# Second-norm adaLN columns on two engines, down projections one up tile later, and unread value products in a two-layer hybrid transformer kernel

## The chip, the cores and the metric

One core of a Trainium2 chip runs the whole program in one launch. The metric is the device time of an execution in microseconds. Before the change three runs took 1842.49, 1840.63 and 1834.53 us: median 1840.63.

## What is computed

One inference step of a diffusion backbone with two layers, for 128 context tokens and 512 latent tokens of width 1024, all in float32. Cut to what matters here, a layer is

```python
sa, ca, ga, sf, cf, gf = silu(cond) @ w_ada + b_ada     # six vectors of 1024, for context and for latents
h = rmsnorm(x) * g_mix * (1 + ca) + sa
q, ckv, krope, qd, kd, vd, u = split(h @ w_in)          # latent attention, differential attention, Fourier
o = concat(mla(q, ckv, krope), diff(qd, kd, vd), fourier(u)) @ w_out
x = x + ga * o
h = rmsnorm(x) * g_ffn * (1 + cf) + sf                  # the second norm
gate, val = split(conv3(h @ w_up))
x = x + gf * (silu(gate) * val) @ w_down
```

In `w_ada` the 6 x 1024 outputs are 48 columns of 128. Columns 0 to 7 are the shift `sa`, 8 to 15 the scale `ca`, 16 to 23 the gate `ga`, 24 to 31 the shift `sf` of the second norm, 32 to 39 its scale `cf`, 40 to 47 the gate `gf`.

## The kernel before

Activations lie feature-major, as tiles of 128 features by up to 646 tokens. A float32 product is made of three matmuls (`mm3`, L130 to L133): both operands are split into a rounded high part and the rest. `weight` (L117 to L125) loads a block of weights through SP's DMA queue into a tile `raw`, of which two rotate, lets ScalarE (ACT) cast the high half (`whi`, L112) and VectorE (DVE) or GpSimd (POOL) subtract the low half (`wlo`, L113). A tile scheduler orders each engine's instructions by priority when the program is built; the engines then run their lists in order. Work under `later(FILL)` has low priority and is placed late, where others leave room.

A layer runs through these stages. `norm_first`, `diff_k` and `diff_q` make the first projections. `diff_v` (L452) makes the values of differential attention: four blocks of weights i, each against five token groups t, into three PSUM tiles `vps`; in the last block each finished group is split into high and low halves `VVd` (ACT cast L431, subtraction L432). The heads follow in a hand-written order, the string `SEQ` (L1058): `d` and `m` are heads, `F` is the Fourier mixing (names `fc`, `fcc`, `fp`, `fpc`), `w0` and `w1` load the first two blocks of `w_out`, and each `g` is one adaLN column on TensorE (PE).

An adaLN column is made in one of three ways. `ada_pe` (L165) loads the column's weights into a `raw` tile and makes eight plain float32 matmuls of 128 columns (`ada2p`, L170; two columns are needed, they are repeated 64 times). `ada_dve` (L146) loads them in another layout into an `ada` tile and makes two multiply-and-sum passes on DVE (L149) and an addition (L152). `ada_pool` (L156) multiplies on POOL (L159), sums on ACT (L160) and adds on DVE (L161). In layer 0 the columns 16 to 23 are the `g` of the heads.

`ffn` (L895) begins with the out projection. For two halves of the tokens and eight blocks m of `w_out` it makes 24 matmuls `wo`, adds the result to x (`residual`, L862) and its squares to `acc_x` for the norm. In layer 0 `step` sends the sixteen columns 24 to 39 along with the blocks, by turns as `ada_dve` and `ada_pool` (`ADA2_ENG`), in numbers given by `ADA2_STEP`. When a half is through, `stats` makes its norm (`rsh`, `rb`), `make_gain` (L177) turns the scale columns 32 to 39 into `gain`, and `modulate` normalises the half (`nt`, `hh_o`, `hl_o`).

Then come 22 up tiles j. Each has two blocks of weights and two halves, 96 matmuls `up`, and a convolution on ACT and DVE (L987, L989), the gate on ACT and POOL, and the split `gh` (ACT), `gl` (POOL). Three further columns per up tile (40 to 47, and all of layer 1) run on DVE. The tiles form the groups `FGROUPS = ((0, 8), (8, 8), (16, 6))`; behind each group come its down products `dn` (L1003 to L1032), the last group's by halves.

```python
SEQ = ('... g g m00 . e2 m01 P m10 F p0 m11 p1 m20 w0 w1 m21 p2', ...)
ADA2_ENG = "VPVPVPVPVPVPVPVP"
ADA2_STEP = (0, 0, 0, 2, 2, 3, 3, 3, 3)
```

Of the kernel before, what the change touches and what calls it, by code (L numbers as in the profile page):

```python
# [21 lines left out]
P = 128  # L22
L = 2
# [22 lines left out]
def backbone_kernel(ctx: ExitStack, tc: tile.TileContext, A, O):  # L46
# [221 lines left out]
    def attention(l, xs, rb, close_x):  # L268
        with tc.tile_pool(name=f"at{l}", bufs=1, side="left", reuse_waits="tile") as ap, \
# [183 lines left out]
            def diff_v():  # L453
                vv = [vvt(f"VVd{p}") for p in range(NPAIR)]
                s0, s1, s2 = sct("vps0"), sct("vps1"), avt("vps2")
                ps = [s0[:, 0:384], s0[:, 512:896], s1[:, 0:384], s1[:, 512:896], s2[:, :384]]
                for i in range(4):
                    hi, lo = weight(A["w_v"][l, i], 768)
                    for t in range(5):
                        for k in (2 * i, 2 * i + 1):  # L460
                            c0 = 132 + 128 * t if t < 4 else 2
                            s = slice(c0, c0 + 128)
                            w = slice(384 * (k % 2), 384 * (k % 2) + 384)
                            mm3(ps[t], hh[k][:, s], hl[k][:, s], hi[:, w], lo[:, w], k == 0, k == NK - 1)
                        if i == 3 and t < 4:
                            v_split(vv, t, ps[t])
# [335 lines left out]
            gates = list(range(16, 24)) if l == 0 else []  # L802
# [88 lines left out]
    def ffn(l, oh, ol, ws):  # L891
        xs, accs, close = x_pool(f"x{l}")
        with tc.tile_pool(name=f"ff{l}", bufs=1, side="left", reuse_waits="tile") as fp, \
# [17 lines left out]
            def ada_list(js, xpool=None, engs=""):  # L911
                scond = ada_cond(fp.tile([P, 2, D], F32, name="scond", tag="scond"))
                junk = fp.tile([P, D], BF16, name="junk", tag="junk")
                if "P" in engs:
                    prod = xpool.tile([P, 2, D], F32, name="prod", tag="prod")

                def step(n):
                    for _ in range(min(n, len(js))):
                        ll, j = js.pop(0)
                        wt = (xpool if xpool and j % 2 else fp).tile([P, D], F32, name="ada", tag="ada", bufs=ADA_BUFS)  # L920
                        if engs[j - 24:j - 23] == "P":
                            ada_pool(ll, j, wt, scond, prod)
                        else:
                            ada_dve(ll, j, wt, scond, junk)
# [46 lines left out]
            for f0, nf in FGROUPS:  # L971
                G = []
                for j in range(f0, f0 + nf):
                    c = []
                    for gv in range(2):
                        wh, wl = weight3(A["w_up"][l, j, gv], 1024)
                        ct = gpl.tile([P, 2, 322], F32, name="cg" if gv == 0 else "cv", tag=f"c{gv}", bufs=2)
                        cw = wconv[:, j, gv]
                        for hf in range(2):
                            t = pst("up")[:, :324]  # L980
                            r = slice(322 * hf, 322 * hf + 324)
                            for k in range(NK):
                                s = slice(128 * k, 128 * k + 128)
                                mm3(t, wh[:, s], wl[:, s], hh[k][:, r], hl[k][:, r], k == 0, k == NK - 1)
                            d = ct[:, hf]
                            nc.scalar.activation(out=d, in_=t[:, 1:323], func=AF.Copy, scale=cw[:, 1:2])
                            nc.vector.scalar_tensor_tensor(out=d, in0=t[:, 0:322], scalar=cw[:, 0:1], in1=d,  # L987
                                                           op0=ALU.mult, op1=ALU.add)
                            nc.vector.scalar_tensor_tensor(out=d, in0=t[:, 2:324], scalar=cw[:, 2:3], in1=d,  # L989
                                                           op0=ALU.mult, op1=ALU.add)  # L990
                        c.append(ct)
                    nc.scalar.activation(out=c[0], in_=c[0], func=AF.Silu)
                    nc.gpsimd.tensor_tensor(out=c[0], in0=c[0], in1=c[1], op=ALU.mult)  # L993
                    gh = gpl.tile([P, 2, 322], F32R, name="gh", tag="gh", bufs=GV_BUFS)
                    gl = gpl.tile([P, 2, 322], F32R, name="gl", tag="gl", bufs=GV_BUFS)
                    hi_lo(gh, gl, c[0], nc.gpsimd)
                    G.append((gh, gl))
                    step(3)
                if f0 + nf == NFF:
                    step(48)  # L1000
                    if l + 1 < L:
                        make_gain(l + 1, 0)
                last = f0 + nf == NFF  # L1003
                for hs in ((0,), (1,)) if last else ((0, 1),):
# [17 lines left out]
                    if last:  # L1022
                        rb[hs[0]] = stats(hs[0], 321, [acc, sq], pool)
                        if l + 1 == L:
                            for k in range(NK):
                                y = pool.tile([P, 642], F32, name="y", tag="t640")
                                for o, w, c, r in rb[hs[0]]:
# [4 lines left out]
                                    nc.sync.dma_start(out=dst, in_=y[:, o:o + w])  # L1032
            if l + 1 < L:
# [14 lines left out]
ADA2_ENG = "VPVPVPVPVPVPVPVP"  # L1048
RAWX = 1
XL = 2  # L1050
ADA2_STEP = (0, 0, 0, 2, 2, 3, 3, 3, 3)
# [6 lines left out]
SEQ = ('q1 d00 d01 k2 q2 K0 B+ . g d10 A+ e0 . d11 g g n0 e1 g d20 K1 n1+ d21 . g n2+ g g . K2 U+ . g g m00 . e2 m01 P m10 F p0 m11 p1 m20 w0 w1 m21 p2', 'd00 q1 d01 k2 q2 K0 d10 g B+ . g g A+ e0 . K1 g d11 e1 n0 g n1+ d20 . n2+ . g K2 g . d21 U+ m00 . g g e2 P m01 m10 F m11 p0 m20 w0 w1 m21 p2 p1')  # L1058
# [66 lines left out]
def _layout(i):  # L1125
# [11 lines left out]
    o["w_ada0"] = wa[0].reshape(NK, P, 48, P).transpose(2, 1, 0, 3)[:24].reshape(24, P, D)  # L1137
# [62 lines left out]
```

## Time and profile before

| | |
|---|---|
| median of three runs | 1840.63 us (1834.53 to 1842.49) |
| profiled execution | 1835.91 us, its span 1834.1 us |
| PE busy, mean granted clock | 1702.3 us (93%), 0.959 |
| DVE, ACT, POOL busy | 1160.6, 779.4, 647.0 us |
| layer 0: value products | about 75 to 105 us |
| layer 0: out projection `wo` | 377.6 to 459.4 us |
| layer 0: up and down products | from 463.9 us |
| layer 1: value products, out projection's end | about 985 to 1015, 1343 us |

The profile is of one execution, and its times are counted from the start of its span. A matmul's listed duration is its latency, since matmuls overlap; the pace is the distance of their starts, or a count over a window. PEclk is the granted clock of TensorE as a share of 2.4 GHz, so 0.5 is its lower level of 1.2 GHz. The idle time in square brackets stands before an instruction, with what ended it. DMA times go from the issue to the landing of the last byte.

### The profile page before, as it was taken

What the parts mean: (1) busy time and instruction counts of PE and PEld (TensorE: products, weight loads), DVE (VectorE), ACT (ScalarE), POOL (GpSimd) and SP (SyncE); (2) the same over time, 40 slices, a digit from 0 to 9 for tenths busy, and PEclk for the clock granted to TensorE, in tenths of its full rate; (3) what the DMA queues carried; (4) which work ended last, traced back from release to release, by engine and by line L of the source; (5) the groups of instructions that cost most, each with busy time, mean ns of one, the idle gap of its engine ahead of it and who ended that gap; (6) DMA issues with size and microseconds to landing.
All of it is one profiled execution on the core that took longest, in us unless ns stands there. A gap on an engine that the chain in (4) does not pass through costs nothing. (4 is left out here: it accounts for less than half of the span.)

```text
span 1834.1 us, 29035 instructions
## 1 busy us (share of the span) xinstructions
PE 1702.3 (93%) x11160; PEld 1653.7 (90%) x11160; DVE 1160.6 (63%) x2051; ACT 779.4 (42%) x1494; POOL 647.0 (35%) x719
## 2 busy tenths in 40 slices
PE   5888899988899999999998888999999999999997
PEld 4878899878799999999987878988999999999997
DVE  8738775679899999634455388765544434443445
ACT  5436665653533123313344457665333313321332
POOL 6547454558432002201232566562312201220222
PEclk8889999998799999999999899999999999999998
DMA  7367754654355665322254566652312222222223
GB/s 276 108 204 216 206 168 135 210 186 160 109 168 173 194 197 172 93 81 70 64 180 142 162 206 192 190 194 64 104 35 81 70 78 72 71 80 70 78 69 119
DMA packets 81084, 249.70 MB, mean 136 GB/s; under 512 B 10417, under 2 KB 19761, under 8 KB 79281
## 3 DMA queue, kind: packets, MB, share of 16 engines
q1 hardware_dynamic: 74226, 209.13, 35.9%
q0 software_dynamic: 6720, 38.72, 7.6%
q8 instruction: 88, 1.44, 0.3%
q14 instruction: 50, 0.41, 0.1%
HBM read 203.43 MB, written 41.24 MB: 133 GB/s over the span
## 5 line engine op out<-in xcount | busy, mean ns | idle before, releaser
L132 PE MATMUL up<-hl_o,whi 128*128 128x324 f32 x1408 | 440.9, 314 | 3.9 <-POOL hl_o L113 3.9
L131 PE MATMUL up<-hh_o,whi 128*128 128x324 f32 x1408 | 440.1, 314 | 2.9 <-ACT hh_o L112 1.7
L133 PE MATMUL up<-hh_o,wlo 128*128 128x324 f32 x1408 | 440.2, 313 | 0.0
L112 ACT CAST whi<-raw 128x1024 fp32r<-128x1024 f32 (+2 forms) x210 | 207.0, 989 | 427.3 <-PE dn L132 201.8
L113 DVE TENSOR_TENSOR wlo<-raw,whi 128x1024 fp32r<-128x1024 f32 (+2 forms) x184 | 225.2, 1228 | 199.4 <-ACT whi L112 195.3
L993 POOL TENSOR_TENSOR cg<-cg,cv 128x644 f32<-128x644 f32 x44 | 72.2, 1640 | 666.9 <-DVE cv L989 646.2
L132 PEld LDWEIGHTS up<-hl_o,whi 128*128 128x128 f32 x1408 | 267.5, 190 | 5.9 <-POOL hl_o L113 5.8
L131 PEld LDWEIGHTS up<-hh_o,whi 128*128 128x128 f32 x1408 | 267.3, 190 | 3.5 <-ACT hh_o L112 2.1
L133 PEld LDWEIGHTS up<-hh_o,wlo 128*128 128x128 f32 x1408 | 266.7, 190 | 0.0
L131 PE MATMUL dn<-gh,whi 128*128 128x322 f32 x704 | 218.0, 313 | 4.8 <-ACT gh L112 3.7
L132 PE MATMUL dn<-gl,whi 128*128 128x322 f32 x704 | 219.8, 313 | 0.0
L133 PE MATMUL dn<-gh,wlo 128*128 128x322 f32 x704 | 218.5, 312 | 0.0
L149 DVE CUSTOM_DVE_ANT_0 junk<-ada,scond 128x1024 bf16<-128x1024 f32 x138 | 195.7, 1418 | 5.3 <-ACT scond L143 2.5
L480 DVE TENSOR_REDUCE nm<-sc 128x1 f32<-128x640 f32 (+1 forms) x180 | 126.5, 711 | 76.6 <-PE sc L579 54.9
L481 ACT ACTIVATE P<-sc,nm 128x640 f32<-128x640 f32 (+1 forms) x180 | 128.4, 715 | 81.9 <-DVE nm L480 60.3
L862 DVE SCALAR_TENSOR_TENSOR x_x<-dn,mods,x_x 128x128 f32<-128x128 f32 (+2 forms) x144 | 57.6, 436 | 130.6 <-PE dn L133 130.4
L131 PEld LDWEIGHTS dn<-gh,whi 128*128 128x128 f32 x704 | 132.6, 189 | 6.7 <-ACT gh L112 4.0
L132 PEld LDWEIGHTS dn<-gl,whi 128*128 128x128 f32 x704 | 133.6, 190 | 0.3 <-POOL gl L113 0.2
L133 PEld LDWEIGHTS dn<-gh,wlo 128*128 128x128 f32 x704 | 133.4, 190 | 0.4 <-DVE wlo L113 0.4
L131 PE MATMUL proj<-hh_n,whi 128*128 128x320 f32 (+1 forms) x320 | 108.7, 340 | 5.3 <-DVE VVm L654 2.5
L132 PE MATMUL proj<-hl_n,whi 128*128 128x320 f32 (+1 forms) x320 | 106.0, 331 | 0.0
L133 PE MATMUL proj<-hh_n,wlo 128*128 128x320 f32 (+1 forms) x320 | 105.6, 330 | 0.0
(299 smaller groups left out, 3706.9 us busy)
## 6 DMA issues: line engine op xcount, KB each, us to landing
raw<-in_w_up SPq DMA_DIRECT2D x88, 512.0 KB, 3.5
ada<-in_w_adaT SPq DMA_DIRECT2D x83, 512.0 KB, 3.7
raw<-in_w_down SPq DMA_DIRECT2D x32, 512.0 KB, 3.6
raw<-in_w_in SPq DMA_DIRECT2D x28, 512.0 KB, 4.5
raw<-in_w_down SPq DMA_DIRECT2D x32, 384.0 KB, 3.2
qs<-dq POOLq DMA_DIRECT2D x12, 865.5 KB, 9.0
ks<-mk POOLq DMA_DIRECT2D x12, 768.0 KB, 5.0
raw<-in_w_out SPq DMA_DIRECT2D x16, 512.0 KB, 4.1
```

Source lines behind the costliest of these rows:

```text
L112: nc.scalar.copy(out=hi, in_=src)
L113: (lo_eng or nc.vector).tensor_tensor(out=lo, in0=src, in1=hi.bitcast(F32), op=ALU.subtract)
L131: nc.tensor.matmul(out, lhsT=lh, rhs=rh, start=first, stop=False)
L132: nc.tensor.matmul(out, lhsT=lh, rhs=rl, start=False, stop=False)
L133: nc.tensor.matmul(out, lhsT=ll, rhs=rh, start=False, stop=last)
L149: nc.vector.tensor_tensor_reduce(out=junk, in0=wt, in1=scond[:, c], op0=ALU.mult, op1=ALU.add, scale=1.0, scalar=0.0, accum_out=mods[:, l, ...
L480: nc.vector.tensor_reduce(out=nm, in_=s_in, axis=ax, op=ALU.max, negate=True)
L481: nc.scalar.activation(out=p_out, in_=s_in, func=AF.Exp, bias=nm, scale=1.0, accum_out=s_out)
L862: nc.vector.scalar_tensor_tensor(out=x[:, o:o + w], in0=ps, scalar=gate, in1=x[:, o:o + w], op0=ALU.mult, op1=ALU.add)
L993: nc.gpsimd.tensor_tensor(out=c[0], in0=c[0], in1=c[1], op=ALU.mult)
```

## The change

The change has three parts.

The second norm's columns in layer 0: 24 to 31 (the shift) leave the out projection and become eight more `g` among the last heads, as `ada_pe`; the input `w_ada0` grows from 24 to 32 columns. 32 to 39 (the scale) stay with the out projection, now all as `ada_dve`, fewer per step. `ada_pool` is no longer called there.

The down products of a group, in both layers, come behind the first up tile of the next group. Those of the last group stay where they were.

In `diff_v`, both layers, seven matmuls of 128x512 whose result is never read (`warm`) stand ahead of the blocks i=2 and i=3. Their operands are the low half of the block before.

```diff
+    def warm(n, lhsT, rhs):
+        t = tpt("warm")[:, :rhs.shape[-1]]
+        for _ in range(n):
+            nc.tensor.matmul(t, lhsT=lhsT, rhs=rhs, start=True, stop=True)
...
+                lo = None
                 for i in range(4):
+                    if i > 1:
+                        warm(7, lo[:, :128], lo[:, :512])
                     hi, lo = weight(A["w_v"][l, i], 768)
...
-            gates = list(range(16, 24)) if l == 0 else []
+            gates = list(range(16, 32)) if l == 0 else []
...
-                    step = ada_list([(l, j) for j in range(24, 40)], wop, ADA2_ENG)
+                    step = ada_list([(l, j) for j in range(32, 40)], wop)
...
-            for f0, nf in FGROUPS:
-                G = []
-                for j in range(f0, f0 + nf):
...
-                if f0 + nf == NFF:
-                    step(48)
-                    if l + 1 < L:
-                        make_gain(l + 1, 0)
...
+            G = {}
+            for f0, nf in FGROUPS:
+                for j in range(f0, f0 + nf):
+                    G[j] = up(j)
+                    step(3)
+                    if j == f0 and f0:
+                        down(f0 - 8, 8, [G.pop(i) for i in range(f0 - 8, f0)])
+            step(48)
+            if l + 1 < L:
+                make_gain(l + 1, 0)
+            down(f0, nf, [G[i] for i in range(f0, NFF)])
...
-ADA2_ENG = "VPVPVPVPVPVPVPVP"
...
-ADA2_STEP = (0, 0, 0, 2, 2, 3, 3, 3, 3)
+ADA2_STEP = (0, 0, 0, 1, 1, 1, 1, 2, 2)
...
-... m00 . e2 m01 P m10 F p0 m11 p1 m20 w0 w1 m21 p2
+... m00 . e2 m01 P g g m10 g F p0 g m11 g p1 g m20 w0 w1 g m21 g p2
...
-    o["w_ada0"] = wa[0].reshape(NK, P, 48, P).transpose(2, 1, 0, 3)[:24].reshape(24, P, D)
+    o["w_ada0"] = wa[0].reshape(NK, P, 48, P).transpose(2, 1, 0, 3)[:32].reshape(32, P, D)
```

`up` and `down` hold the code of before, moved into functions. Where the scheduler put things shows in the built order of the engines. Line numbers of the changed kernel are 6 to 9 higher than before from `ada_dve` on.

PE at the end of layer 0's attention, first before, then changed. `av` and `avc` are the last head's products, `fp` is Fourier, `ada2p` adaLN columns, `wo` the out projection.

```order
L545 MATMUL av<-th,VVm_3083 128x256
L553 MATMUL avc<-th,VVm_3083 128x128
L546 MATMUL av<-tl,VVm_3083 128x256
L554 MATMUL avc<-tl,VVm_3083 128x128
L131 MATMUL wo<-hh_o_3462,whi 128x322
L132 MATMUL wo<-hl_o_3470,whi 128x322
L133 MATMUL wo<-hh_o_3462,wlo 128x322
```

```order
L133 MATMUL fp<-tb,yl 128x256
L131 MATMUL fp<-tb,rowh 128x256
L132 MATMUL fp<-tb,rowh 128x256
L133 MATMUL fp<-tb,rowl 128x256
L176 MATMUL ada2p<-c_condT,raw 128x128 x32
L131 MATMUL wo<-hh_o_3490,whi 128x322
L132 MATMUL wo<-hl_o_3498,whi 128x322
L133 MATMUL wo<-hh_o_3490,wlo 128x322
```

Four of the new columns (32 matmuls) and the last Fourier products now stand between the heads and the out projection. The other four stand among the last heads.

SP, the queue of loads, at the same place, first before, then changed. `raw<-in_w_out` are the weights of the out projection, `raw<-in_w_ada` those of columns on PE, `ada<-in_w_adaT` those of columns on DVE, `x_x` the residual.

```order
L121 DMA raw<-in_w_in 128x1024
L167 DMA raw<-in_w_ada 128x1024
L121 DMA raw<-in_w_out 128x1024
L641 DMA mk_170<-base 128x1x768 x2
L121 DMA raw<-in_w_out 128x1024 x3
L929 DMA x_x_4277<-in_xT 128x642
L929 DMA x_x_4278<-in_xT 128x642
```

```order
L933 DMA x_x_4396<-in_xT 128x642
L173 DMA raw<-in_w_ada 128x1024
L915 DMA wconv<-in_w_conv 128x132
L148 DMA scond<-in_cond 128x2048
L153 DMA ada<-in_w_adaT 128x1024 x2
L121 DMA raw<-in_w_out 128x1024
L153 DMA ada<-in_w_adaT 128x1024 x2
L173 DMA raw<-in_w_ada 128x1024
L121 DMA raw<-in_w_out 128x1024
L153 DMA ada<-in_w_adaT 128x1024 x3
L121 DMA raw<-in_w_out 128x1024
L173 DMA raw<-in_w_ada 128x1024
```

Before, four loads of `w_out` stood ahead of the residual's eight loads. Now all eight stand behind them, in turn with columns' loads, and the last column's load stands behind the second block of `w_out` through `raw`.

PE in `diff_v` at the last block of weights, first before, then changed.

```order
L133 MATMUL vps_669<-whi,hl_n_183 128x384
L131 MATMUL vps_669<-whi,hh_n_176 128x384
L132 MATMUL vps_669<-wlo,hh_n_176 128x384
L133 MATMUL vps_669<-whi,hl_n_184 128x384
L131 MATMUL vps_667<-whi,hh_n_177 128x384
L132 MATMUL vps_667<-wlo,hh_n_177 128x384
L133 MATMUL vps_667<-whi,hl_n_185 128x384
```

```order
L133 MATMUL vps_669<-whi,hl_n_183 128x384
L131 MATMUL vps_669<-whi,hh_n_176 128x384
L132 MATMUL vps_669<-wlo,hh_n_176 128x384
L133 MATMUL vps_669<-whi,hl_n_184 128x384
L139 MATMUL warm<-wlo 128x512 x7
L131 MATMUL vps_667<-whi,hh_n_177 128x384
L132 MATMUL vps_667<-wlo,hh_n_177 128x384
L133 MATMUL vps_667<-whi,hl_n_185 128x384
```

The seven unread matmuls stand ahead of the block's first product; the same is found ahead of i=2, and twice in layer 1.

## Rows read from the trace of the kernel before

**Rows 1.** The page, section 1: engine, busy us (share of the span), instructions.

```profile
PE 1702.3 (93%) x11160; PEld 1653.7 (90%) x11160; DVE 1160.6 (63%) x2051; ACT 779.4 (42%) x1494; POOL 647.0 (35%) x719
```

**Rows 2.** Windows: width; PE, PEld, DVE, ACT, POOL busy (count); PEclk, DMA, GB/s.

```profile
500.00:598.00 98.00, 98.00 (x659) 98.00 (x658) 98.00 (x159) 35.26 (x55) 23.68 (x14) 1.00 0.56 174
```

**Rows 3.** PE waits from 75, 985, 370, 500, 620: total, times, longest.

```profile
PE vps L131 <- DVE VVd L432: 3.9, 1, 3.9
...
PE vps L131 <- DVE VVd L432: 4.6, 1, 4.6
...
PE wo L133 <- DVE wlo L113: 5.8, 2, 3.3
...
PE dn L131 <- ACT gh L112: 3.7, 1, 3.7
...
PE dn L131 <- ACT whi L112: 0.6, 3, 0.2
```

**Rows 4.** Windows in the value products of layers 0 and 1.

```profile
80.00:90.00 10.00, 10.00 (x56) 9.66 (x55) 4.12 (x3) 2.84 (x3) 8.39 (x7) 1.00 0.88 243
100.00:105.00 5.00, 3.12 (x11) 2.64 (x11) 1.36 (x5) 2.29 (x8) 1.47 (x3) 0.65 0.93 352
1015.00:1020.00 5.00, 5.00 (x24) 5.00 (x25) 0.29 (x1) 0.79 (x4) 3.89 (x6) 0.67 0.51 158
```

**Rows 5.** PE in order of time, `wo`: start, us, operation [idle before].

```profile
377.62 0.36 PE L131 MATMUL wo<-hh_o,whi 128*128 128x322 f32 x1
...
459.12 0.30 PE L133 MATMUL wo<-hh_o,wlo 128*128 128x320 f32 x1
```

**Rows 6.** Windows in and behind the out projections of layers 0 and 1.

```profile
400.00:420.00 20.00, 16.69 (x93) 16.43 (x94) 20.00 (x21) 6.38 (x11) 17.55 (x9) 0.84 0.61 197
460.00:480.00 20.00, 12.71 (x42) 10.19 (x43) 15.15 (x38) 13.38 (x38) 15.20 (x20) 0.55 0.30 106
1340.00:1350.00 10.00, 6.97 (x40) 6.75 (x40) 6.64 (x15) 4.06 (x8) 1.61 (x2) 0.83 0.00 0
```

**Rows 7.** Window around the first down products of layer 0.

```profile
605.00:615.00 10.00, 7.55 (x40) 7.55 (x41) 9.01 (x14) 2.83 (x3) 3.38 (x2) 0.83 0.43 141
```

**Rows 8.** PE in order of time, value products of layer 0.

```profile
94.41 0.33 PE L133 MATMUL vps<-whi,hl_n 128*128 128x384 f32 x1
98.61 0.69 PE L131 MATMUL vps<-whi,hh_n 128*128 128x384 f32 x1 [3.87 <-DVE VVd L432]
...
102.30 0.52 PE L133 MATMUL vps<-whi,hl_n 128*128 128x384 f32 x1
```

**Rows 9.** ACT in order of time, same place.

```profile
95.78 1.04 ACT L112 CAST whi<-raw 128x1024 fp32r<-128x1024 f32 x1 [8.61 <-DMA raw<-in_w_in]
96.73 0.26 ACT L431 CAST VVd<-vps 128x128 fp32r<-128x128 f32 x1
```

**Rows 10.** PE in order of time, an adaLN column among the heads.

```profile
343.79 0.66 PE L170 MATMUL ada2p<-c_condT,raw 128*128 128x128 f32 x4
344.21 0.40 PE L131 MATMUL sc<-ks,qs 128*128 128x320 f32 x1
```

**Rows 11.** SP (DMA issues) in order of time, around the out projection.

```profile
344.48 6.34 SPq L121 DMA_DIRECT2D raw<-in_w_out  x2
...
382.00 2.27 SPq L121 DMA_DIRECT2D raw<-in_w_out  x3
```

**Rows 12.** DMA issues, whole span, then 375-392: KB, median us to landing.

```profile
raw<-in_w_up SPq DMA_DIRECT2D x88, 512.0 KB, 3.5
...
raw<-in_w_out SPq DMA_DIRECT2D x3, 512.0 KB, 7.1
```

**Rows 13.** Groups by line, 368-485: busy us, mean ns, idle before.

```profile
L159 POOL TENSOR_TENSOR prod<-ada,scond 128x1024 f32<-128x1024 f32 x16 | 46.9, 2944 | 0.8 <-ACT prod L160 0.8
...
L149 DVE CUSTOM_DVE_ANT_0 junk<-ada,scond 128x1024 bf16<-128x1024 f32 x23 | 37.9, 1647 | 2.6 <-ACT scond L143 2.5
```

**Rows 14.** DVE in order of time, end of the out projection.

```profile
461.11 0.57 DVE L161 TENSOR_SCALAR mods<-mods,c_b_ada 128x2 f32<-128x2 f32 x1 [3.47 <-ACT prod L160]
```

More of the change, by code (lines that the diff above doesn't have):

```diff
@@ L909, in pst, with ada_list @@
                 return pf.tile([P, 512], F32, name=nm, tag="f", bufs=6)
-            def ada_list(js, xpool=None, engs=""):
+            def ada_list(js, xpool=None):
                 scond = ada_cond(fp.tile([P, 2, D], F32, name="scond", tag="scond"))
                 junk = fp.tile([P, D], BF16, name="junk", tag="junk")
-                if "P" in engs:
-                    prod = xpool.tile([P, 2, D], F32, name="prod", tag="prod")
                 def step(n):
@@ L920, in step @@
                         wt = (xpool if xpool and j % 2 else fp).tile([P, D], F32, name="ada", tag="ada", bufs=ADA_BUFS)
[L921 to L924, printed above, removed]
+                        ada_dve(ll, j, wt, scond, junk)
                 return step
@@ L970, in ffn @@
             acc = accs()
-            for f0, nf in FGROUPS:
-                G = []
-                for j in range(f0, f0 + nf):
[L974 to L998, printed above, removed]
-                if f0 + nf == NFF:
-                    step(48)
-                    if l + 1 < L:
-                        make_gain(l + 1, 0)
@@ new lines, in up @@
+            def up(j):
+                c = []
+                for gv in range(2):
+                    wh, wl = weight3(A["w_up"][l, j, gv], 1024)
+                    ct = gpl.tile([P, 2, 322], F32, name="cg" if gv == 0 else "cv", tag=f"c{gv}", bufs=2)
+                    cw = wconv[:, j, gv]
+                    for hf in range(2):
+                        t = pst("up")[:, :324]
+                        r = slice(322 * hf, 322 * hf + 324)
+                        for k in range(NK):
+                            s = slice(128 * k, 128 * k + 128)
+                            mm3(t, wh[:, s], wl[:, s], hh[k][:, r], hl[k][:, r], k == 0, k == NK - 1)
+                        d = ct[:, hf]
+                        nc.scalar.activation(out=d, in_=t[:, 1:323], func=AF.Copy, scale=cw[:, 1:2])
+                        nc.vector.scalar_tensor_tensor(out=d, in0=t[:, 0:322], scalar=cw[:, 0:1], in1=d,
+                                                       op0=ALU.mult, op1=ALU.add)
+                        nc.vector.scalar_tensor_tensor(out=d, in0=t[:, 2:324], scalar=cw[:, 2:3], in1=d,
+                                                       op0=ALU.mult, op1=ALU.add)
+                    c.append(ct)
+                nc.scalar.activation(out=c[0], in_=c[0], func=AF.Silu)
+                nc.gpsimd.tensor_tensor(out=c[0], in0=c[0], in1=c[1], op=ALU.mult)
+                gh = gpl.tile([P, 2, 322], F32R, name="gh", tag="gh", bufs=GV_BUFS)
+                gl = gpl.tile([P, 2, 322], F32R, name="gl", tag="gl", bufs=GV_BUFS)
+                hi_lo(gh, gl, c[0], nc.gpsimd)
+                return gh, gl
@@ L1003, in ffn, with down @@
+            def down(f0, nf, G):
                 last = f0 + nf == NFF
```

2 lines of the change are left out of this document (1 added, 1 removed).

## The prediction

> **What bounds the kernel.** I read the page's shares first, then TensorE's waits, then the stages that hold them in windows and in order of time. PE is busy 93% of the span [rows 1] at a mean granted clock of 0.959, and in the up projections of layer 0 it never stops: 659 matmuls in 98 us at clock 1.00, 0.149 us each, with VectorE (DVE) busy all 98 us beside it [rows 2]. So time lies only where PE waits, and where it runs at the lower level of its clock (1.2 instead of 2.4 GHz) after a wait. The change touches three such places. In the value products of the two layers PE waits 3.9 and 4.6 us for the DVE split of the first results [rows 3], and the windows behind show clocks of 0.65 and 0.67 [rows 4]. In layer 0's out projection and the norm behind it PE does little: the 384 `wo` matmuls need 57 us at the pace of [rows 2] and take 81.8, from 377.62 to 459.4 [rows 5]; then 460 to 480 holds 42 PE instructions at clock 0.55 [rows 6], where 134 would fit. Near 607 PE waits 3.7 us for the last gated tile of a group [rows 3].
>
> The sum is made against the profiled execution: 1835.91 us, of which the span is 1834.1. It lies 4.7 us under the median of the three runs, 1840.63; the forecast below is the median plus the sum.
>
> **Down projections one up tile later.** In layer 0 the first down products wait 3.7 us for `gh` [rows 3], which ScalarE (ACT) casts behind DVE's convolution, and the ten microseconds around the wait show clock 0.83 [rows 7]: some 3.4 us at half clock, 1.7 us lost. With a whole up tile between (96 matmuls, 14 us by [rows 2]) `gh` is long there, and the ten buffers of `gh` hold the eight tiles of the group and the next. At the other group ends of both layers PE's list of waits has none over 0.2 us [rows 3], so nothing is to be had there: **-5.4 us**. If DVE is so far behind that the extra up tile finds no free PSUM tile, the wait only moves: 0 at worst.
>
> **Unread products.** Seven 128x512 matmuls stand ahead of i=2 and of i=3, 14 per layer. None of their size is in the trace. PE is full through these products: 56 of 128x384 in 10 us [rows 4], one every 0.179, so by columns 512 take 0.24 us: an estimate of 3.3 us per layer, 6.6 if the clock were half. They push the end of the third product group from 94.74 to 98.1, and PE's wait of 3.87 ended at 98.61 [rows 8]. What sets that end? Not PE: ACT, which works in order, sat 8.6 us on the `raw` tile of the next projection's weights, cast it at 95.78, and only then made the first VVd cast at 96.73 [rows 9]; DVE's split and PE follow. The order of ACT is unchanged up to there, and so is what that transfer waits for. (On SP the third load behind it now stands ahead of the cached values' load; ACT comes to those only when the next projection runs.) So the 3.3 us run out inside the old wait: 0.5 us of it stays in layer 0, 1.2 of 4.6 in layer 1. Nothing is won by that alone; the gain is the clock. After the wait 12 matmuls start every 0.335 us (98.61 to 102.30 and the next, [rows 8]) instead of 0.179: 1.9 us, and as much in layer 1, where 1015 to 1020 still has clock 0.67 and holds 24 matmuls where 34 of 0.149 fit [rows 4]: 1.5 more. At most -5.3; I take **-4**, near that end, because only an eighth and a quarter of the old waits is left in front. The other end is +6.6 for both layers, if the transfer lands early enough that the products delay everything behind them.
>
> **Columns of the second norm.** Eight columns of 8 matmuls go to PE. The four matmuls from 343.79 to 344.21 start 0.105 us apart [rows 10], so a column is 0.85 us, eight are 6.8. Four stand among the last heads; I let none of their time hide in PE's short waits there: +3.4 (0 if all did). The Trainium skill, page "TensorE: Matmul & The Clock Gate", section "Wait — 56ns, not 53.3ns?", has matmuls of 128 columns start 55.6 ns apart at full clock; by that page, as an estimate, the four columns would cost 1.8 and not 3.4. The trace does not agree for these float32 operands, and its row decides.
>
> The other four stand between the last Fourier product and the first `wo` product, and this is the costly point, since the weights of `wo` come through the same two `raw` tiles, in turn with the columns' weights. Before, four of the eight `w_out` loads went out from 344.48 on, well ahead [rows 11]. Now they follow the columns' loads, each of which waits until PE or DVE is done with the tile's old content. From the end t0 of the Fourier products: two columns have their weights. The third's load is issued at about t0+1 among five other loads of 512 KB; in before three such `w_out` loads, issued from 382.00 to 384.27 behind three columns, took a median of 7.1 us [rows 11, 12], so that the third landed some 9.4 us after the first went out, and three more stand ahead here: t0+12. The first `w_out` lands with it, is cast, and its low half stands on DVE behind three to four columns of 2 x 1.65 us [rows 13], which start when the first column's own load is there, about t0+5 (between 3.5 and 7.1): t0+16.5. Only then is a tile free for the fourth column: load 3.5 us [rows 12], eight matmuls at half clock 1.7: first `wo` at **t0+22**. The near bound is t0+15 (every transfer at the 3.5 us of the up weights), the far one t0+27 (each at the 7.1).
>
> t0 is 377.6 + 3.4 for the columns - 1.8 from layer 0's value products + some 3 for Fourier pieces that now come last and no longer fill the heads' waits (no row has this; I take it between 0 and the 5.8 us of the largest entry of [rows 3]): 382. `wo` starts at 404 instead of 377.62.
>
> What comes back: the waits inside `wo`. It lost 24.7 us, 5.8 of it in waits for `wlo` [rows 3], with DVE busy 20 of 20 and the clock at 0.84 from 400 to 420 [rows 6]; now POOL has no products (16 of 2.94 us, [rows 13]), and the weights land during the front wait, while DVE has its eight columns of this list as before and the next list's behind them. I allow 3 us: `wo` ends at 404 + 57 + 3 = 464, +4.6. Then the transition. In before gain comes behind the last POOL column, L161 at 461.11, for which DVE had waited 3.47 us [rows 14], so the first half was not modulated before `wo` was over; now gain's scale columns are there before `wo` ends and the first half is modulated under `wo`. The second half still has its own chain, with some eight half columns between on DVE. Before lost about 15 us here (42 instructions are 6.3 of the 20 us, and 1.3 more around them); layer 1, without columns, lost 4.0 (40 instructions, 6.0 us, in the 10 from 1340, [rows 6]). I take 11, two thirds of the way up, for DVE's columns: -4. Together **0**, between -16 (front t0+15, transition as layer 1) and +19 (front t0+27, `wo` keeps half its old waits, transition as before).
>
> **Sum:** -5.4 - 4 + 0 = -9.4 on 1835.91, so 1826.5 in a profiled run and about **1831** as a median.
>
> **Rivals.** (A) *Slower: the front wait is not earned back.* The loads take 7 us each as in [rows 12], `wo` starts at t0+27 = 409, and DVE, still full of columns, keeps 12 of the old 24.7 us: `wo` ends at 478, transition as before: +19 - 9.4 = +9.6, 1850. It decides from a `wo` start past about 405. For it: SP issues in order, so one late load holds all behind it, and DVE was full here before [rows 6]. Against: POOL's products, which slow DVE's, are gone. (B) *Faster: stage and transition run clean.* Front t0+15, no waits in `wo`, transition as layer 1's 4.0: -16 - 9.4 = -25, 1815; half of that 1823. For it: layer 1 runs the same code with a loss of 4.0. Against: layer 1 has no columns. (C) *The unread products are not hidden*, or the clock falls all the same: +6.6 instead of -4 gives +1, 1842. For it: ACT's wait was for a transfer [rows 9], which need not take as long again. Against: nothing in the change touches what is in flight beside it. (D) *The down wait only moves*: -4, 1837; against it, the order of ACT and POOL behind the up tile.
>
> **Numbers.** Forecast 0.42, with 8 us either way for the front wait and the transition: half of it beyond 0.5% faster. A 0.23, mostly slower by over 0.5%. B 0.23, nearly all faster. C 0.07 and D 0.05, no change. About 0.5% (9.2 us) is what a measurement of this kernel can tell from no change. Faster 0.44, same 0.37, slower 0.19. The range reaches from B's end to a little past A: 1816 to 1852; the forecast case alone is 1823 to 1839.
>
> **What would show it.** Right: the `vps` wait at 98 under 1 us with the clock at 1.00 behind it; no `dn <- gh` wait near 607; PE idle some 20 us ahead of the first `wo` with the chain through `raw<-in_w_ada`, then `wo` in about 60 us and no wait for the gain. Wrong: `wo` starting within 10 us of 382 (then B), waits of several us inside `wo` for `wlo` (then A), the first VVd cast later than 96.7 (then C), or a new wait in the up tile after a group (then D).

## The result, and the profile after

The changed kernel is slower, by 1.3%. Four runs have a median of 1862.48 us (1860.73 to 1865.09), four runs of the kernel before beside them 1838.36 (1834.53 to 1842.49): a ratio of 1.0127, interval 1.0091 to 1.0164. The prediction said 1831, and 1852 at most. The profiled span grew from 1834.1 to 1859.0 us, by 24.9.

The page of the changed kernel, section 1, answers to [rows 1]: PE is busy 19 us longer, the other three engines 16 to 42 us less, so it is PE that must be followed.

```profile
PE 1721.7 (93%) x11316; PEld 1675.0 (90%) x11316; DVE 1140.2 (61%) x2051; ACT 762.9 (41%) x1462; POOL 604.6 (33%) x703
```

Of PE's 156 new instructions 28 are the unread products. The other 128 are the eight columns: each of a column's eight plain float32 matmuls stands in the trace as two, so a column is 16 of them.

Marks on PE's list in order of time, the first or last product of each stage, say where the 25 us came from:

| stretch on PE | before, us | after, us | change |
|---|---|---|---|
| layer 0, to the first product of the heads (`projw`) | 104.7 | 102.9 | -1.8 |
| layer 0, heads, to the end of the last `avc` | 273.1 | 278.1 | +5.0 |
| layer 0, from there to the first `wo` | -0.2 | 40.1 | +40.3 |
| layer 0, first to last `wo` | 81.5 | 61.4 | -20.1 |
| layer 0, norm, up and down, to the last `dn` | 499.3 | 498.2 | -1.1 |
| layer 1, first value product to the first product of the heads | 32.1 | 29.7 | -2.4 |
| layer 1, heads | 263.9 | 267.9 | +4.0 |
| layer 1, the rest, and the passage from layer 0 | | | +1.0 |

**Value products.** PE's waits of the changed kernel from 75 and from 1010 us (total, times, longest) answer to the first two of [rows 3]:

```profile
PE vps L131 <- DVE VVd L438: 0.5, 1, 0.5
...
PE vps L131 <- DVE VVd L438: 0.8, 1, 0.8
```

Its windows (width; busy us and count of PE, PEld, DVE, ACT, POOL; PEclk, DMA share, GB/s) in the value products of both layers, in `wo` of layer 0, and from its end to the steady up products, answer to [rows 4, 6]:

```profile
95.00:105.00 10.00, 7.65 (x45) 7.04 (x44) 2.92 (x11) 5.41 (x17) 4.77 (x7) 1.00 0.95 320
1015.00:1035.00 20.00, 17.31 (x94) 16.09 (x92) 4.34 (x12) 7.41 (x19) 8.66 (x8) 1.00 0.99 294
421.16:482.85 61.69, 59.68 (x406) 59.42 (x406) 56.28 (x113) 25.72 (x55) 23.91 (x40) 0.99 0.62 198
482.85:504.30 21.45, 11.28 (x55) 10.74 (x54) 20.15 (x36) 4.25 (x11) 11.17 (x9) 0.68 0.37 122
```

The waits of 3.9 and 4.6 us are 0.5 and 0.8, and the clock is 1.00 behind them, where it was 0.65 and 0.67 [rows 4]. ACT in order of time answers to [rows 9]: the same wait for the same load, and the first VVd cast 0.04 us later than before.

```profile
95.81 1.05 ACT L112 CAST whi<-raw 128x1024 fp32r<-128x1024 f32 x1 [8.43 <-DMA raw<-in_w_in]
96.77 0.26 ACT L437 CAST VVd<-vps 128x128 fp32r<-128x128 f32 x1
```

**From the heads to the out projection.** PE in order of time (start, us, operation, idle before it and what ended that):

```profile
380.81 0.22 PE L563 MATMUL avc<-tl,VVm 128*128 128x128 f32 x1
...
394.90 0.41 PE L133 MATMUL fp<-tb,rowl 1*128 1x256 f32 x1
396.83 3.75 PE L176 MATMUL ada2p<-c_condT,raw 128*128 128x128 f32 x16 [1.51 <-DVE x L770]
400.89 2.54 PE L176 MATMUL ada2p<-c_condT,raw 128*128 128x128 f32 x16 [0.31 <-DVE mods L178]
405.49 2.02 PE L176 MATMUL ada2p<-c_condT,raw 128*128 128x128 f32 x16 [2.06 <-DMA raw<-in_w_ada]
417.75 3.75 PE L176 MATMUL ada2p<-c_condT,raw 128*128 128x128 f32 x16 [10.24 <-DMA raw<-in_w_ada]
421.16 0.61 PE L131 MATMUL wo<-hh_o,whi 128*128 128x322 f32 x1
```

The last head ends at 381, the last Fourier product 14 us behind it, and the first `wo` starts 26 us behind that. In before all three lay within 3 us: the Fourier products had been done at 375.0, ahead of the last head's, and `wo` followed the last head at once [rows 5]. The window of the 14 us, columns as above:

```profile
381.04:395.31 14.27, 10.89 (x60) 9.87 (x60) 3.55 (x7) 3.08 (x7) 1.33 (x1) 0.75 0.23 79
```

Fourier's 60 matmuls, which in before ran among those of the heads, keep PE busy for 10.9 us, and it waits 3.4 us between them. SP's issues behind it, and DVE's split of the first `w_out` block, show what the 10.24 us wait is:

```profile
400.61 0.33 SPq L173 DMA_DIRECT2D raw<-in_w_ada  x1
403.46 0.33 SPq L121 DMA_DIRECT2D raw<-in_w_out  x1
406.22 5.66 SPq L153 DMA_DIRECT2D ada<-in_w_adaT  x3
411.98 0.37 SPq L121 DMA_DIRECT2D raw<-in_w_out  x1
414.08 0.33 SPq L173 DMA_DIRECT2D raw<-in_w_ada  x1
...
412.84 1.22 DVE L113 TENSOR_TENSOR wlo<-raw,whi 128x1024 fp32r<-128x1024 f32 x1
```

The last column's load goes out at 414.08, behind the second `w_out` block (411.98). It needs the `raw` tile of the first block, which was asked for at 403.46 and which DVE, busy with columns of its own, splits only from 412.84 to 414.05. So 3.7 us of the wait are the load, the rest is the turn of the tile. The column's matmuls at 417.75 then hold back `wo`, whose first weights are ready.

**Out projection and behind.** The third window above is `wo`: PE busy 59.7 of 61.7 us at clock 0.99, where it was 0.84 from 400 to 420 [rows 6]. The fourth is the norm and the passage to the up products: 55 matmuls in 21.5 us at clock 0.68. The three waits that make it, on PE in order of time:

```profile
490.08 0.38 PE L235 MATMUL rsh<-ones,acc_x 128*128 128x1 f32 x2 [4.56 <-POOL acc_x L225]
...
496.61 1.54 PE L246 MATMUL rsh<-ident,rb 128*128 128x128 f32 x6 [2.70 <-DVE rb L243]
...
501.06 0.91 PE L131 MATMUL up<-hh_o,whi 128*128 128x324 f32 x2 [2.92 <-ACT hh_o L112]
```

At the end of the first group the wait of [rows 3] is still there, in two pieces and one up tile later. PE's waits from 500 to 660:

```profile
PE dn L131 <- ACT gh L112: 1.8, 1, 1.8
PE dn L132 <- POOL gl L113: 1.3, 1, 1.3
```

The heads, finally, take 5.0 and 4.0 us longer. The code of layer 1's heads did not change at all.

### The profile page after: what moved, and what is told of

The parts are those of the page before. It is cut to its first block, busy times and chain, and to the rows that moved or that the text cites. A ratio compares the mean times of both kernels' runs of the same rounds, so it can differ in the third digit from the quotient of the medians.

```text
span 1859.0 us, 29315 instructions
## 1 busy us (share of the span) xinstructions
PE 1721.7 (93%) x11316; PEld 1675.0 (90%) x11316; DVE 1140.2 (61%) x2051; ACT 762.9 (41%) x1462; POOL 604.6 (33%) x703
## 5 line engine op out<-in xcount | busy, mean ns | idle before, releaser
L995 POOL TENSOR_TENSOR cg<-cg,cv 128x644 f32<-128x644 f32 x44 | 78.3, 1779 | 663.0 <-DVE cv L991 584.3
L155 DVE CUSTOM_DVE_ANT_0 junk<-ada,scond 128x1024 bf16<-128x1024 f32 x138 | 187.0, 1355 | 5.5 <-ACT scond L149 2.7
L113 DVE TENSOR_TENSOR tl<-tp,th 128x512 fp32r<-128x512 f32 x144 | 87.9, 618 | 32.1 <-ACT th L112 30.7
```

The costliest lines, as they stand in the source:

```text
L113: (lo_eng or nc.vector).tensor_tensor(out=lo, in0=src, in1=hi.bitcast(F32), op=ALU.subtract)
L155: nc.vector.tensor_tensor_reduce(out=junk, in0=wt, in1=scond[:, c], op0=ALU.mult, op1=ALU.add, scale=1.0, scalar=0.0, accum_out=mods[:, l, ...
```

## The experiments

Two theories run through the expectations, each of which says what it holds of its kernel. By the first, the whole loss lies with the columns, which stand in the way of Fourier and of the out projection, and the other parts do as forecast. By its rival, an edit also moves the order that the scheduler gives the heads, and the heads pay for it. Each part was first made alone.

### The columns alone

```diff
-            gates = list(range(16, 24)) if l == 0 else []
+            gates = list(range(16, 32)) if l == 0 else []
...
-                    step = ada_list([(l, j) for j in range(24, 40)], wop, ADA2_ENG)
+                    step = ada_list([(l, j) for j in range(32, 40)], wop)
...
-ADA2_STEP = (0, 0, 0, 2, 2, 3, 3, 3, 3)
+ADA2_STEP = (0, 0, 0, 1, 1, 1, 1, 2, 2)
...
-... m00 . e2 m01 P m10 F p0 m11 p1 m20 w0 w1 m21 p2
+... m00 . e2 m01 P g g m10 g F p0 g m11 g p1 g m20 w0 w1 g m21 g p2
```

> The first part alone on the kernel before: eight more columns on TensorE, eight on VectorE; no unread products, down products where they were. Theory Q (turns): the new columns take turns in one PSUM tile with the Fourier products and in the two raw tiles with w_out, so Fourier ends some 14 us behind the last head and the first wo some 26 us behind Fourier; wo itself runs in about 61 us. This part alone then makes +22 to +30 us on 1838, all of the loss and a little more. Rival W (unread products): the loss comes from the unread products and from the order of the heads that they bring; then this part alone is within 8 us of before.

Measured: 1868.63 us against 1840.12, ratio 1.0164 (1.0142 to 1.0185). In layer 0 the last head ends at 371.5, Fourier 20 us behind, `wo` starts 26 us behind that, and the `wo` products take 64.8 us. That is 28.5 us, more than the whole loss of 24.1: beside this part the other two take some of it back, though without it, as shown below, they cost 6.3. But layer 1, untouched by this part, has slow heads too: 275.1 us against 263.9. Its window (columns as above):

```profile
1035.49:1310.61 275.12, 248.67 (x1611) 232.60 (x1612) 184.51 (x344) 158.66 (x370) 145.92 (x172) 0.91 0.53 161
```

The same 1611 matmuls take 11.3 us longer at clock 0.91 instead of 0.95. So part 1 is the main loss, and the order of the heads has its first evidence.

### The down projections alone

```diff
+                for j in range(f0, f0 + nf):
+                    G[j] = up(j)
+                    step(3)
+                    if j == f0 and f0:
+                        down(f0 - 8, 8, [G.pop(i) for i in range(f0 - 8, f0)])
```

> The second part alone on the kernel before: down products one up tile later. Theory B (backlog): the wait for gh near 607 goes and leaves none, -5 us, as was forecast; in the changed kernel it came back only because the first part put VectorE's columns elsewhere. Rival M (moves): VectorE is behind by more than an up tile, so a wait for gh of 1 to 3 us and a stretch of half clock stay, and the time is within 2 us of before.

Measured: 1832.37 us, ratio 0.996 (0.9946 to 0.9975), 7.7 us faster. From the last `wo` to the last `dn` of layer 0 it takes 492.8 us instead of 499.3. The window in which before waited for `gh` is full, and the whole stretch has clock 1.00:

```profile
605.00:622.00 17.00, 17.00 (x116) 17.00 (x115) 17.00 (x29) 4.21 (x6) 3.26 (x2) 1.00 0.57 186
486.30:960.80 474.50, 470.91 (x3163) 469.58 (x3161) 358.84 (x603) 152.90 (x228) 93.20 (x112) 1.00 0.43 140
```

PE has no wait for `gh` or `gl` left there. The part does by itself what was forecast for it, and a little more. PE's order in the heads is the same as in before, row for row.

### The unread products alone

```diff
+                lo = None
                 for i in range(4):
+                    if i > 1:
+                        warm(7, lo[:, :128], lo[:, :512])
                     hi, lo = weight(A["w_v"][l, i], 768)
```

> The third part alone on the kernel before: 14 unread matmuls per layer in the value products. In both layers the wait at the third product group goes and the next projection starts 1.8 to 2.4 us earlier, so -4 us if nothing else changes. Rival H (heads): the changed order of the heads costs layer 1 4 us (as seen in the changed kernel, 34 instead of 24 us of half clock in its attention), and the time is within 2 us of before.

Measured: 1856.26 us, ratio 1.0087 (1.007 to 1.0104). By the marks of the table above they win 1.2 and 2.2 us in the value products, and the heads behind them then take 11.3 and 10.0 us more. Windows of the heads, layers 0 and 1, of the kernel before:

```profile
104.70:377.79 273.09, 251.04 (x1739) 237.88 (x1740) 176.88 (x352) 160.54 (x369) 142.79 (x172) 0.95 0.59 181
1014.84:1278.69 263.85, 238.97 (x1611) 224.12 (x1612) 179.54 (x344) 159.43 (x370) 145.90 (x172) 0.95 0.55 168
```

and of this one:

```profile
103.46:387.86 284.40, 258.57 (x1739) 244.61 (x1740) 185.68 (x352) 159.23 (x369) 144.13 (x172) 0.93 0.57 176
1024.80:1298.70 273.90, 247.30 (x1611) 232.16 (x1612) 184.16 (x344) 159.16 (x370) 146.93 (x172) 0.92 0.54 164
```

The work is the same, 1739 and 1611 matmuls, but its order is not. In PE's list as the traces have it, with columns and unread products left out and equal neighbours counted once, a layer's heads have some 1370 rows; 395 rows in layer 0 and 505 in layer 1 have to be taken out or put in to make the one list of the other. So it is the order that differs, or else the unread products themselves disturb what follows. The next two kernels tell these apart.

### Down projections and unread products

Both edits above together.

> The second and third part on the kernel before, the first undone. Theory Q: the whole loss is the first part's, so this kernel is 2 to 10 us faster than before: -9 if both parts do as forecast, -4 to -5 if one of them. Rival W: this kernel is as slow as the changed one or at least 10 us slower than before.

Measured: 1846.46 us, ratio 1.0039 (1.0024 to 1.0055), 6.3 us slower, which neither theory had. The heads take 284.5 and 274.0 us, as with the unread products alone, whose order they share; the down projections keep their gain. The two add up: +16.1 and -7.7 give +8.4, and +6.3 was measured.

### One unread product, and ten

```diff
-                        warm(7, lo[:, :128], lo[:, :512])
+                        warm(1, lo[:, :128], lo[:, :512])
```

> The third part alone with one unread matmul in place of seven: 2 per layer, half a microsecond. Theory O (order): what the unread products cost is that the scheduler, whose planned times shift, puts the heads behind them in another order, and most orders are worse than the one of before. Here the built order of the heads is again another one in layer 0, and in layer 1 it is that of the changed kernel. O says +4 us in layer 1's heads as there, +5 to +12 in layer 0's, so +8 to +16 in all, for half a microsecond of work. Rival W (the products themselves): a seventh of the 16 us of seven, so within 3 us of before.

Measured: 1855.98 us, ratio 1.0084 (1.0067 to 1.0101): four unread matmuls in the whole program cost 15.5 us. That is what theory O said. PE's order differs from before by 391 and 610 rows. The heads, 8.9 and 11.1 us longer (in layer 1 only 4 were expected):

```profile
104.33:386.32 281.99, 258.10 (x1739) 243.43 (x1740) 184.08 (x352) 159.61 (x369) 144.19 (x172) 0.94 0.56 176
1025.85:1300.78 274.93, 246.16 (x1611) 231.61 (x1612) 185.35 (x344) 160.40 (x370) 144.06 (x172) 0.92 0.52 161
```

```diff
-                        warm(7, lo[:, :128], lo[:, :512])
+                        warm(10, lo[:, :128], lo[:, :512])
```

> The third part alone with ten unread matmuls in place of seven: 20 per layer, 4.8 us, more than the wait that they stand in. The built order of the heads is almost that of before in both layers (55 of some 2450 rows apart in layer 0, 113 in layer 1). Theory O: the heads cost within 2 us of before in both layers, and the value products gain 0 to 2 us each, so -4 to +2 in all. Rival W: ten times 2.3 us, some +20 us.

Measured: 1837.78 us, ratio 0.9986 (0.9972 to 1.0001). Forty unread matmuls cost nothing. The order differs by 53 rows in layer 0 and 96 in layer 1, counted as above (a layer's list has some 1370 rows, not the 2450 of the expectation). The heads, 1.4 and 3.8 us longer than before, where within 2 was expected:

```profile
104.77:379.29 274.52, 253.70 (x1739) 240.55 (x1740) 177.64 (x352) 160.59 (x369) 142.31 (x170) 0.94 0.59 180
1016.14:1283.78 267.64, 243.50 (x1611) 227.77 (x1612) 182.33 (x344) 159.67 (x370) 144.42 (x170) 0.94 0.55 165
```

Four cost 15.5 us, 28 cost 16.1, forty none. The number of products and their time do not explain that; the order does. The traces of all twelve kernels bear it out. They hold five orders of layer 1's heads, whose 1611 matmuls no edit touches:

| rows of PE's list apart from before | kernels | layer 1's heads, us |
|---|---|---|
| 0 | before; down projections alone | 263.9, 262.1 |
| 96 | ten unread; down projections and ten unread; columns earlier; weights ahead of the columns | 267.6, 264.7, 263.7, 262.2 |
| 486 | columns alone | 275.1 |
| 505 | seven unread; down projections and seven unread; Fourier ahead of the columns | 273.9, 274.0, 272.6 |
| 610 | changed kernel; one unread | 267.9, 274.9 |

The first two orders have a mean of 264.0 us, the other three one of 273.1, and on both sides stand kernels with the new columns and kernels with unread products. One list alone spreads by up to 7 us, each time being that of one execution. Why the order changes was not followed step by step; that the scheduler works from planned times, which a shift ahead of the heads moves, is the obvious reading.

### The columns earlier among the heads

If the columns' place is what costs, the same eight columns, named early in the string, must free Fourier and the out projection.

```diff
-... B+ . g d10 A+ e0 . d11 g g n0 e1 g d20 K1 n1+ d21 . g n2+ g g . K2 U+ . g g m00 . e2 m01 P g g m10 g F p0 g m11 g p1 g m20 w0 w1 g m21 g p2
+... B+ . g g d10 A+ e0 . d11 g g g g n0 e1 g g d20 K1 n1+ d21 . g g n2+ g g g g . K2 U+ . g g g m00 . e2 m01 P m10 F p0 m11 p1 m20 w0 w1 m21 p2
```

> The first part alone, but the eight new columns stand two by two with the old ones in the early heads, ahead of the Fourier products and of the w_out loads. Theory Q (turns in the shared PSUM tile and the two raw tiles): Fourier ends with the last head again, the first wo follows it at once and runs some 20 us shorter than before, so the time is below before's in spite of 7 us of new matmuls: -16 to -2, the width being the order of the heads. Rival C (columns): the loss of the first part comes from making these columns on TensorE at all and from VectorE's share; then it stays at +10 or more.

Measured: 1857.75 us, ratio 1.0092 (1.0068 to 1.0115): 17 us slower where 2 to 16 faster were expected. The end of the stage did nearly as expected: Fourier ends 6.8 us behind the last head, `wo` follows it at once and takes 63.1 us, 18 less than before, and layer 1's heads take 263.7. The loss went into layer 0's heads, 36 us more than before. Their window, then PE's waits in them:

```profile
104.43:413.57 309.14, 270.41 (x1841) 254.81 (x1842) 181.58 (x357) 159.79 (x365) 141.73 (x171) 0.92 0.54 168
```

```profile
PE proj L131 <- ACT whi L112: 7.9, 5, 2.5
PE proj L133 <- POOL wlo L113: 4.5, 2, 2.9
```

PE now waits for the weights of the heads' projections, which come through the same two `raw` tiles as the columns': 12.4 us, where before has one such wait of 2.3. A column costs its turn in `raw`, and in the early heads that turn is taken from a projection. That is some 10 of the 36 us. Its matmuls cost as well: the window holds 102 matmuls more than before's, at about 0.11 us some 11 us. At clock 0.92 about 49 us of it are at half clock where before had 27, which loses another 11.

### Weights of the out projection ahead of the columns

```diff
-... m01 P g g m10 g F p0 g m11 g p1 g m20 w0 w1 g m21 g p2
+... m01 P w0 w1 g g m10 g F p0 g m11 g p1 g m20 g m21 g p2
```

> The first part alone, but the first two w_out loads come ahead of the new columns in the turn for the raw tiles; the Fourier products still come behind columns in the turn for the PSUM tile. Theory Q: Fourier still ends some 20 us behind the last head, but the wait from there to the first wo falls from 26 to 8 to 14 us; layer 1's heads have almost the order of before, so they give back 11. In all +28.5 - 14 - 11, so 0 to +10 over before. Rival S (the loads are slow whoever is first): the front wait stays over 20 us and the time at +15 or more.

Measured: 1854.78 us, ratio 1.007 (1.0048 to 1.0092). The first two blocks of `w_out` are there early, and still `wo` starts 22.0 us behind Fourier's end, where 8 to 14 were expected and the rival had over 20, and Fourier ends 20 us behind the last head. Layer 1's heads take 262.2 us, back at the level of before. (The profiled execution took 1847.84 us, the other three 1854.34 to 1855.62.) PE's waits from 360 to 445:

```profile
PE ada2p L176 <- DVE mods L178: 6.2, 2, 5.9
PE ada2p L176 <- DMA raw<-in_w_ada: 3.0, 1, 3.0
```

The load of a column costs only 3 us here; instead a column waits 5.9 us for DVE to empty the PSUM tile of the column before. So early weights alone do not free `wo`: with the columns standing last, one shared thing or another holds them.

### Fourier ahead of the columns

Columns, projections and Fourier products (`fcc`, `fpc`, `fc`, `fp`) share one PSUM tile, which they fill in program order:

```python
def mmt(nm):
    return pp.tile([P, 512], F32, name=nm, tag="mm", bufs=1)
```

If a column of low priority, named ahead of `F`, holds Fourier back through that tile, then naming `F` ahead of the new columns sets Fourier free and leaves more columns behind it.

```diff
-... m01 P g g m10 g F p0 g m11 g p1 g m20 w0 w1 g m21 g p2
+... m01 P m10 F p0 g g g g m11 g p1 g m20 w0 w1 g m21 g p2
```

> The first part alone, with the Fourier products ahead of all new columns in the turn for the PSUM tile; the columns still ahead of the w_out loads. One look, for the trace of layer 0. Theory Q: Fourier runs among the last heads again and ends at most 4 us before or behind the last head's products instead of 20 us behind; seven columns are left behind it, so the wait from the last Fourier product to the first wo grows from 26 to 35 us or more. Rival L (the columns' low priority or their load puts Fourier off wherever it stands): Fourier still ends 14 us or more behind the last head.

Measured, in a single run: 1873.07 us. Fourier ends 6.6 us behind the last head instead of 20, outside both ranges but nearer to the up to 4 expected of the tile than to the rival's 14 or more. The first `wo` comes 42 us behind Fourier's end. PE's waits from 360 to 445:

```profile
PE ada2p L176 <- DMA raw<-in_w_ada: 16.6, 4, 10.6
PE ada2p L176 <- DVE mods L178: 3.6, 2, 3.3
```

What is won at Fourier is lost at the columns: they still take turns with each other and with `w_out`. The shared PSUM tile fits this, but a second buffer for it, which alone would show it, was not tried.

### Down projections and ten unread products

The two parts that cost nothing in the heads, together.

> The second part and ten unread matmuls in place of seven; the columns as before. The built order of the heads is that of the ten alone. Theory O: down products -7.7 and ten unread -2.6, as each measured by itself, add up to -10, so 1828 to 1833, the fastest here. Rival P (parts disturb each other, as seven unread and the second part did where the sum of 16 and -8 was 8 and 6 came out): then -3 to +3.

Measured: 1830.95 us (1827.89 to 1840.71), ratio 0.9958 (0.9929 to 0.9988). It beats both kernels, by 8.3 us before and by some 30 the changed one. It cannot be told apart from the down projections alone (0.996).

## Why the prediction was wrong

The forecast for a profiled run was 1826.5 us and 1860.73 was measured, 34 us more. Some 19 of these had come up by the end of layer 0's `wo`; 8 lie in the transition and the down projections, 4 in layer 1's heads, 1 elsewhere. A further 2.4 are an error in the sum: the 1.8 us that layer 0's value products gain are taken off t0, and so are in the +4.6 at the end of `wo`, and are taken off again in the -4; and +4.6 - 4 was rounded to 0.

**Unread products, in their place: right.** Forecast -4, measured -1.8 and -2.4, by the steps named: a product took 0.23 us (0.24 estimated; before's trace does have 128x512 matmuls, eight `swap`, though of another kind), the 3.3 us ran out inside the old wait, the first VVd cast came at 96.77 as before, 0.5 and 0.8 us of wait were left (0.5 and 1.2 forecast), and the clock stayed at 1.00.

**Front wait: mis-sized, but within its bounds.** Forecast t0+22, between t0+15 and t0+27; measured 26 us, through the chain that was named, `raw<-in_w_ada` behind two blocks of `w_out` and behind the split that DVE's columns hold back. The wait for the last column's load was the largest piece, 10.24 us; the load went out 2.3 us later than forecast. The price of a column was wrong by half: 0.85 us was worked out for eight matmuls 0.105 us apart, but the four instructions of [rows 10] are two matmuls of the program, and a column is 16 such instructions. The third column took 2.02 us at clock 1.00, the first and the last 3.75 at 0.50 instead of the 1.7 of the sum. So eight columns are some 14 us of PE and not 6.8. The Trainium skill's 55.6 ns between matmuls of 128 columns (page "TensorE: Matmul & The Clock Gate", section "Wait — 56ns, not 53.3ns?") would, as an estimate, make 16 of them 0.9 us at the higher level; this trace again does not agree for these operands.

**t0: the step that failed most.** "Some 3 for Fourier pieces that now come last" was 14.3, from 381.04 to 395.31. The bound of 5.8, taken from a wait of another kind, was no bound. The built order showed the Fourier products behind the last head, and I priced them as loose pieces. They are a chain of 60 matmuls and of DVE splits, which had run among the heads' products and now ran alone, with 3.4 us of waits and at a clock of 0.75. The experiment that names Fourier ahead of the columns speaks for the shared PSUM tile as the reason (20 us become 6.6). `wo` ended at 482.85 instead of 464. Of these 18.9 us, 11.3 are Fourier, 1.8 the heads, 4 the front wait and 1.7 `wo`.

**`wo`: right.** 60 us forecast, 61.7 measured. Of 24.7 us of waits 20 were earned back.

**Transition: -4 forecast, about -2 measured.** 55 matmuls at 0.149 us are 8.2 of 21.5 us, so 13 are lost, where before lost about 15 and 11 were forecast. The scale columns and gain were no longer in the way, but the wait for `acc_x` (4.56), for `rb` and for `hh_o` were.

**Down projections: -5.4 forecast, nothing measured.** Rival D, given 0.05, came true in the whole kernel, though not in the part alone (-6.5 in this stretch). The up tile in between did its work on PE, but DVE was a whole up tile behind. The group's last up products had ended at about 613.6; DVE's convolution of them ended near 629, ACT cast `gh` at 632.2, and PE waited 1.8 and 1.3 us and then ran at clock 0.51 from 634.0 to 640.9. With the columns alone the old waits for `gh` grew to 4.9 us in all. Without part 1, in the three kernels with the down projections that keep the columns as before, there is no such wait. So part 1 brings it to the changed kernel; by which of DVE's instructions was not taken apart, and the old wait also grew, to 5.2 us, with the unread products alone.

**The heads: no term at all.** +5.0 and +4.0 were in no term, beside 3.4 allowed for four columns in layer 0. I had compared the built order only around the edits, taking the heads as the same. In layer 0 the +5.0 hides more. Four columns came into this window and about as many Fourier matmuls left it, 1742 in all for 1739; with the columns alone the same window takes 266.9 us, so the order that comes with the unread products costs about 11 there, as it does by itself. In layer 1 the +4.0 is less than the spread of one list and shows little by itself; the table of the five orders carries the reading. Unread products alone cost 10 to 11 us per layer. About half of this is the clock in layer 0, most of it in layer 1. By the windows' PEclk, 273.09 us at 0.95 hold about 27 us at half clock, 284.40 at 0.93 about 40 (width times one minus PEclk, doubled); 13 us more at half speed are some 6.5 lost. PE's idle time grew by 3.8. In layer 1 the same sum gives some 26 and 44 us, so 9 of the 10.0 lost; idle time grew by 1.7.

The rivals missed as well. A had the sign and the place, a front that is not earned back, but not the way: it kept 12 us of waits in `wo`, of which 4.5 are left, and with 1850 it lacked Fourier, the heads and D.

What stays open is which feature of the order costs the time. With seven unread products six projections of layer 0 stand as one block of 24 matmuls, where before has three such blocks and splits the others by a head's products. But with one unread product there are three as well, and layer 1's slow orders have five or two where before has five, so this is not it. Nor is the order everything: the changed kernel and the one with one unread product have the same order in layer 1, and take 267.89 and 274.93 us. Windows of the changed kernel's heads:

```profile
102.92:381.04 278.12, 253.41 (x1742) 240.93 (x1742) 181.62 (x348) 155.06 (x360) 142.51 (x171) 0.94 0.58 178
1034.78:1302.67 267.89, 241.51 (x1611) 227.34 (x1612) 181.96 (x344) 160.36 (x370) 144.79 (x172) 0.94 0.55 167
```

Its clock is 0.94 there, the other's 0.92. Why the same list is granted a different clock was not tried.

## What to carry to other kernels

Where a scheduler sets the order, an edit is never local: compare the built order of everything behind the edit, also of stages whose code did not change, and measure a version that shifts the plan without doing the edit's work (one unread product, ten) before crediting or blaming the edit. Low-priority work that shares a rotating tile with the main path takes its turn in program order and holds the main path back; price it by the turns of every tile that it passes, loads and PSUM alike, and not by its matmuls alone. Count a step's instructions in a trace before taking its price from their pace: here a matmul of the program was two. And make each part alone: here the down projections gain 0.4%, the unread products gain in their place and lose by the order, and the columns hide the first gain.

## What the runs showed of the hardware that I had not expected

Waits of PE of little more than 1 us can be followed by half clock. In layer 1's heads of before a wait of 1.17 us at 1267.07 stands between these two windows; ahead of it the clock is 1.00, behind it 0.50:

```profile
1255.00:1266.00 11.00, 10.33 (x80) 9.39 (x78) 6.84 (x14) 5.81 (x15) 1.60 (x2) 1.00 0.37 104
1267.07 0.38 PE L545 MATMUL av<-th,VVm 128*128 128x256 f32 x1 [1.17 <-ACT th L112]
1267.50:1274.00 6.50, 5.55 (x24) 4.83 (x24) 2.80 (x6) 2.33 (x6) 1.48 (x2) 0.50 0.01 5
```

So waits among the heads can cost more than themselves. The same 1611 matmuls of layer 1's heads ran at a mean granted clock of 0.95, 0.94, 0.92 and 0.91 in 263.9, 267.6, 273.9 and 275.1 us: the lower the clock, the longer, though not strictly, as 262.2 us at 0.94 in another kernel show. That level is not fixed by the instructions, since one list was granted 0.94 in one kernel and 0.92 in another, for 7 us.

A plain float32 matmul of 128 columns stands in the trace as two instructions: the 16 of a column took 2.02 us at clock 1.00 and 3.75 at 0.50 behind 396.83 of the changed kernel.
